# Weight sums of a fast matrix product, formed by adding transfers in device memory instead of on the vector engine, with larger buffer pools and a refitted order of work

## The chip, the cores and the metric

The kernel runs on one core of one Trainium2 chip. The core has five engines with instruction streams of their own: TensorE (PE; its weight loads are listed as PEld), VectorE (DVE), ScalarE (ACT), GpSimd (POOL) and SyncE (SP). SP does nothing here but issue transfers. Transfers issued from SP and ACT go through hardware queues, those from POOL through a software queue; the profile keeps them apart as q1/q10 and q0. The metric is the device time of one execution in microseconds (us). Before the change, three runs gave 1059.16 to 1060.96 us with a median of 1059.97 us.

## The reference

One layer of a bidirectional encoder on 512 tokens of width 1024, all in float32. Two branches read the same normalised input: a gated linear recurrence (RG-LRU, 12 blocks of 128 channels) and a chunked gated delta rule (DeltaNet, 8 heads, with a 64x64 triangular solve in each chunk). Sigmoid gates merge them, and a SwiGLU feed-forward of width 2816 follows.

```python
h = rmsnorm(x, mix_norm)
rx, ry, qkv, z, ba, gates = split(h @ w_in)                 # 1024 x 9248
y_rnn = rglru_branch(rx, ry, ...) @ w_rnn_proj
y_dn  = deltanet_branch(qkv, z, ba, ...) @ w_dn_proj
g_rnn, g_dn = split(sigmoid(gates))
x = x + (g_rnn * y_rnn + g_dn * y_dn) @ w_out
gt, up = split(rmsnorm(x, ffn_norm) @ w_gate_up)             # 1024 x 5632
x = x + (silu(gt) * up) @ w_down                             # 2816 x 1024
return rmsnorm(x, final_norm)
```

The change touches `w_down` above all, and the places where buffers are shared.

## The kernel before, in words

**Precision.** Matrix products run in a one-pass format. Each operand is split into a high part (ACT casts it) and a low part (DVE subtracts it from the original); a product is three matmuls, high by high, high by low and low by high. So every 512 KB block of weights is loaded into a tile `wraw`, cast on ACT into `whi` and subtracted on DVE into `wlo` before PE can use it. Small products of the DeltaNet branch run in plain float32.

**Stages.** In order of time: the norm of the input; the twelve RG blocks (`rg_front`, `rg_mid`, `rg_out`), in which each block also needs four 128x128 gate weights, loaded into a tile `graw` with one buffer; from about 200 to 650 us the DeltaNet pairs g = 0..3 (`dn_front`, `dn_mats`, `dn_inverse`, `dn_state`, `dn_out`), with other projections between them; the output projection; the feed-forward's gate and up products (`gate_up`, about 720 to 950 us); and the down product to the end (`down_first`, `down_second`).

**The fast products.** `gate_up` and the down product use a seven-product scheme on 2x2 blocks (Strassen's, in Winograd's form), which needs sums of weight blocks. For the down product two of them are formed early: for each j of 11, `b11 + b12` and `b12 + b22`. `down_sums(j)` (L1167) loads 512 KB into `bg` and 256 KB into `bgb`, makes two DVE additions of 128x512, and stores the 512 KB result into a DRAM tile `sums[j]`; `down_first(j)` loads it again much later. These calls stand in the loop over `gate_up`.

**The order of work.** Nothing is issued while the functions run. Every operation is recorded (`Rec`, L384, which is why nearly all profile rows carry that line) with its data dependences, a planner's cost and a wished time. `Plan.order` (L145) then walks through a list schedule of the five engines: at each step an engine takes the ready operation of the earliest wished time whose buffers are free. The wished time is the start of the operation's stage, read from the table `TIMES`, plus an offset within the stage. What stands on the chip is the resulting order per engine; there each engine works strictly in that order and waits where it must. Buffers come from shared pools: `two()` of 2 KB per partition (N2 = 14), `four()` of 4 KB (N4 = 22), and NW = 3 `wraw` tiles; `whi` and `wlo` have two each.

**DeltaNet, as far as it is needed.** `dn_mats(g)` reads decays back from DRAM (`t<-gcr`) and masks them on POOL (AFFINE_SELECT); DVE multiplies them into the matrices `na`. `dn_inverse(g)` inverts 32x32 blocks on DVE by a chain of some 60 tiny operations and three transposes; the first 32x32 matmuls (`ax<-t,na`) need its end. `dn_state(g)` runs four chained steps; POOL scales its keys (TENSOR_SCALAR `t<-t,dnse`).

**The tail.** The last matmuls are split into halves of 256 columns, one into an `ax` bank and one into an `st` bank; DVE adds each to the result, squares are summed, the row norm is formed, and the last rows are scaled and written.

Of the kernel before, what the change touches and what calls it, by code (L numbers as in the profile page):

```python
# [8 lines left out]
F32R = mybir.dt.float32r  # L9
AF = mybir.ActivationFunctionType  # L10
ALU = mybir.AluOpType
# [3 lines left out]
P = 128  # L15
D = 1024
# [10 lines left out]
NF = D_FF // P  # L27
# [5 lines left out]
RELEASE = 200  # L33
LOOK = 40
TIMES = [
# [15 lines left out]
]  # L51
ENGINES = ("PE", "DVE", "ACT", "POOL", "SP")
N2, N4, NW = 14, 22, 3
AHEAD = 12.0
LASTK = 3
GATES = (0, 2, 4, 6, 16)
# [333 lines left out]
def trunk(ctx: ExitStack, tc: tile.TileContext, x, mix_norm, w_in, rg_conv_w, rg_conv_b, rg_wa, rg_ba, rg_wx, rg_bx,  # L390
# [3 lines left out]
    plan = Plan(nc)  # L394
    V, A, G, T = Rec(plan, "DVE", nc.vector), Rec(plan, "ACT", nc.scalar), Rec(plan, "POOL", nc.gpsimd), Rec(plan, "PE", nc.tensor)
    Q = Rec(plan, "SP", nc.sync)
# [3 lines left out]
    wp = ctx.enter_context(tc.tile_pool(name="wp", bufs=2))  # L400
# [5 lines left out]
    dr = ctx.enter_context(tc.tile_pool(name="dr", bufs=1, space=DRAM))  # L406
# [4 lines left out]
    def nm(s):  # L411
        uid[0] += 1
        return f"{s}{uid[0]}"

    def new(pool, shape, tag, bufs, dt=F32):
        return plan.tile(pool, shape, dt, tag, bufs, nm(tag))
# [4 lines left out]
    def axb():  # L421
        return new(ps, (P, 512), "ax", 3)
# [4 lines left out]
    def two(dt=F32, shape=(P, 512)):  # L427
        return new(t2, shape, "t2", N2, dt)

    def four(dt=F32, shape=(P, 2, 512)):  # L430
        return new(t4, shape, "t4", N4, dt)
# [7 lines left out]
    def act(out_, in_, func, after=(), **kw):  # L439
        plan.extra = after  # L440
        A.activation(out_, in_, func, **kw)
        plan.extra = ()

    def spend(us=0.0):
        plan.base += us
        plan.t = plan.base
        plan.stage += 1

    def f(ap):
        return ap.bitcast(F32)  # L450
# [112 lines left out]
    def pcol(i, j):  # L563
        return par[:, i, j:j + 1]
# [85 lines left out]
    def split(src, pair):  # L650
        A.copy(pair[:, 0, :], src)
        V.tensor_tensor(pair[:, 1, :], src, f(pair[:, 0, :]), ALU.subtract)
# [83 lines left out]
    wx = rg_wx[0].rearrange("d n k j -> k n d j")  # L736
    yr = [None] * NB

    def rg_front(b):
        u, us, r, i = two(), four(F32R), four(), four()  # L740
        po = in_proj(C_RX + b * P, admit=(u, us, r, i))
        graw, ghi, glo = new(wp, (P, 4, P), "graw", 1), two(F32R, (P, 4, P)), two(F32R, (P, 4, P))
        now = plan.t
        plan.t = now - (40 if b > 2 else 12)
        Q.dma_start(graw[:, 0:2, :], wa[:, b])
        Q.dma_start(graw[:, 2:4, :], wx[:, b])
        plan.t = now - AHEAD
        A.copy(ghi, graw)
        V.tensor_tensor(glo, graw, f(ghi), ALU.subtract)
        plan.t = now  # L750
        conv(po, lambda k: rg_w(k, b), rg_b(b), u)
        split(u, us)
        for q in range(4):
            d = q % 2
            pq = axb()
            T.matmul(pq, ghi[:, q, :], us[:, 0, :], start=True, stop=False)
            T.matmul(pq, ghi[:, q, :], us[:, 1, :], start=False, stop=False)
            T.matmul(pq, glo[:, q, :], us[:, 0, :], start=False, stop=True)
            act((r if q < 2 else i)[:, d, :], pq, AF.Sigmoid, bias=pcol(0, (O_BA if q < 2 else O_BX) + 12 * d + b))
        V.tensor_tensor(i, i, u.unsqueeze(1).to_broadcast([P, 2, S]), ALU.mult)  # L760
        return r, i
# [402 lines left out]
    wdn = w_down[0].rearrange("(j h p) n -> p j h n", p=P, h=2)  # L1164
    sums = {}

    def down_sums(j, after):  # L1167

        now = plan.t
        r, b22 = new(wp, (P, 2, 512), "bg", 2), new(wp, (P, 512), "bgb", 2)  # L1170
        plan.extra = after
        Q.dma_start(r, wdn[:, j, 0, :].rearrange("p (h n) -> p h n", h=2))
        Q.dma_start(b22, wdn[:, j, 1, 512:D])
        plan.extra = ()
        V.tensor_tensor(r[:, 0, :], r[:, 0, :], r[:, 1, :], ALU.add)
        V.tensor_tensor(r[:, 1, :], r[:, 1, :], b22, ALU.add)
        sums[j] = new(dr, (P, 2, 512), "sums", NF // 2)
        Q.dma_start(sums[j], r)
        plan.t = now

    gates = [(rnn_gate, n) for n in range(KD)] + [(dn_gate, n) for n in range(KD)]
    for g in range(4):
        spend()
        dn_mats(g)
        spend()
        dn_inverse(g)
        spend()
        dn_state(g)
        if g < 3:
            dn_z(g)  # L1190
        spend()
        dn_out(g)
        if g < 3:
            dn_front(g + 1)
        if g == 2:
            dn_z(3)
        for fn, n in gates[GATES[g]:GATES[g + 1]]:
            fn(n)
# [9 lines left out]
    for n in range(KD):  # L1208
# [1 line left out]
        y = four(F32R)  # L1210
        split(mixs[n // 2][:, n % 2, :], y)
        mh.append(y)
    last_split = (len(plan.ops) - 1,)
    spend()


# [95 lines left out]
    BRIDGE = 2  # L1312
# [88 lines left out]
        V.tensor_tensor(fa[n // 2][:, n % 2, :], s_, u, ALU.mult)  # L1401

    for n in range(BRIDGE, NF):
        if n - BRIDGE < NF // 2:
            down_sums(n - BRIDGE, last_split)
        gate_up(n)


# [220 lines left out]
```

## Time and profile before

| | before |
|---|---|
| median of three runs | 1059.97 us |
| the profiled execution: its time, from first to last instruction | 1059.7 us |
| mean granted TensorE clock | 0.997 |
| busy PE / DVE / ACT / POOL | 1044.6 / 872.0 / 676.7 / 56.0 us |
| instructions PE / DVE / ACT / POOL | 6731 / 1606 / 1244 / 109 |
| moved by transfers | 122.83 MB |
| transfers of `down_sums` | 11 of 512 KB, 11 of 256 KB, 11 stores of 512 KB |

The program runs on one core, so there is no other core to compare with. A busy PE is not a PE at its peak: the ends of matmuls are modelled and each row includes the pipeline behind it, so a wait shorter than about that pipeline does not show as idle time. The view of waits names, for each engine, the instruction whose end released it.

### The profile page before, as it was taken

How to read it: one execution, taken by the hardware profiler on the slowest of the kernel's cores; microseconds unless marked ns; L12 is line 12 of the kernel's file. 1: busy time of each engine (PE TensorE's matmuls, PEld its weight loads, DVE VectorE, ACT ScalarE, POOL GpSimd, SP SyncE). 2: the span in 40 equal slices, each digit the busy share in tenths (PEclk: the TensorE clock that was granted, in tenths of full speed). 3: DMA queues.
4: the chain of work that ended last, by engine and by line, in shares of the span. 5: the costliest groups of instructions: out<-in, count | busy, mean ns of one | idle time of the engine just before them, and what ended most of it. 6: DMA issues, size and time to landing. Idle time of an engine off the chain costs nothing.

```text
span 1059.7 us, 17669 instructions
## 1 busy us (share of the span) xinstructions
PE 1044.6 (99%) x6731; PEld 909.9 (86%) x6731; DVE 872.0 (82%) x1606; ACT 676.7 (64%) x1244; POOL 56.0 (5%) x109
## 2 busy tenths in 40 slices
PE   8999999999999999999999999999999999999997
PEld 7888887888879887988888798889999999998786
DVE  7679899769876796599489657679999988989998
ACT  7897997887454766874865535447454454545664
POOL 2000000202000230020010000000000000000000
PEclk9999999999999999999999999999999999999999
DMA  8233232233530352224203314566585342435642
GB/s 239 61 109 90 81 104 75 70 110 91 143 94 23 90 148 81 70 60 110 57 20 95 86 33 147 167 211 224 179 249 160 101 119 81 120 100 192 206 139 100
DMA packets 174389, 122.83 MB, mean 116 GB/s; under 512 B 5952, under 2 KB 160720, under 8 KB 174304
## 3 DMA queue, kind: packets, MB, share of 16 engines
q1 hardware_dynamic: 172832, 118.41, 37.4%
q10 hardware_dynamic: 1184, 3.15, 0.8%
q8 instruction: 53, 0.87, 0.4%
q0 software_dynamic: 288, 0.13, 0.1%
q14 instruction: 32, 0.26, 0.1%
HBM read 113.78 MB, written 7.90 MB: 115 GB/s over the span
## 4 chain that ended last, share of the span: by engine, by line
PE 79%; ACT 8%; DVE 7%; DMA 3%; issue 2%; POOL 0%; SPq 0%; DVEq 0%; ACTq 0%; POOLq 0%
PE mm L384 49%; PE ax L384 20%; PE st L384 11%; ACT t L384 5%; DVE t L384 4%; ACT L384 2%; DVE na L384 1%; ACT whi L384 1%; DVE wlo L384 1%; DMA wraw<-in_w_in_dram 1%; DMA wraw<-in_w_gate_up_dram 0%; ACT ax L384 0%; DMA t<-in_x_dram 0%; DMA wraw<-in_w_down_dram 0%; DMA graw<-in_rg_wx_dram 0%
## 5 line engine op out<-in xcount | busy, mean ns | idle before, releaser
L384 DVE TENSOR_TENSOR t<-t,t 128x512 fp32r<-128x512 f32 (+19 forms) x466 | 227.7, 500 | 19.1 <-ACT t L384 10.8
L384 PE MATMUL mm<-hh,whi 128*128 128x512 f32 (+2 forms) x648 | 230.0, 364 | 0.4 <-ACT hh L384 0.3
L384 PE MATMUL mm<-hl,whi 128*128 128x512 f32 (+2 forms) x648 | 229.4, 363 | 0.8 <-DVE hl L384 0.8
L384 ACT CAST whi<-wraw 128x1024 fp32r<-128x1024 f32 (+3 forms) x139 | 129.9, 936 | 129.8 <-PE mm L384 79.1
L384 DVE TENSOR_TENSOR wlo<-wraw,whi 128x1024 fp32r<-128x1024 f32 (+3 forms) x138 | 150.1, 1088 | 70.0 <-ACT whi L384 31.7
L384 PE MATMUL mm<-hh,wlo 128*128 128x512 f32 (+1 forms) x632 | 147.0, 363 | 0.0
L384 PE MATMUL ax<-t,t 32*32 32x32 f32 (+3 forms) x1062 | 140.8, 285 | 1.6 <-issue 1.1
L384 PEld LDWEIGHTS mm<-hl,whi 128*128 128x128 f32 (+1 forms) x648 | 122.0, 188 | 17.9 <-DVE hl L384 1.2
L384 PEld LDWEIGHTS mm<-hh,whi 128*128 128x128 f32 (+1 forms) x648 | 122.0, 188 | 17.8 <-ACT hh L384 0.5
L384 PEld LDWEIGHTS ax<-t,t 128*128 128x128 f32 (+1 forms) x1062 | 109.4, 159 | 19.6 <-issue 2.9
L384 PEld LDWEIGHTS mm<-hh,wlo 128*128 128x128 f32 x632 | 109.1, 189 | 17.3
L384 ACT CAST t<-t 128x512 fp32r<-128x512 f32 (+2 forms) x128 | 81.9, 652 | 49.2 <-DVE t L384 47.3
L384 PE MATMUL mm<-t,t 128*128 128x256 f32 (+1 forms) x468 | 91.3, 336 | 0.1
L384 ACT ACT_TABLE_LOAD x69 | 88.5, 1283 | 3.1 <-PEq L1615 1.7
L384 DVE SCALAR_TENSOR_TENSOR t<-mm,par,t 128x511 f32<-128x511 f32 (+1 forms) x108 | 79.3, 743 | 10.3 <-ACT t L384 9.1
L384 PE MATMUL mm<-t,whi 128*128 128x512 f32 x320 | 83.4, 396 | 0.5 <-ACT whi L384 0.5
L384 PEld LDWEIGHTS mm<-t,t 128*128 128x128 f32 x468 | 72.7, 190 | 9.3 <-DVE t L384 0.5
L384 PEld LDWEIGHTS mm<-t,whi 128*128 128x128 f32 x320 | 59.2, 188 | 13.5 <-ACT whi L384 1.1
L384 ACT ACTIVATE t<-t 128x128 f32<-128x128 f32 (+4 forms) x86 | 47.1, 558 | 27.7 <-DVE t L384 26.2
L384 ACT CAST t<-wraw 128x1024 fp32r<-128x1024 f32 (+1 forms) x51 | 44.9, 881 | 20.8 <-DMA wraw<-in_w_gate_up_dram 11.3
L384 DVE TENSOR_TENSOR t<-wraw,t 128x1024 fp32r<-128x1024 f32 (+1 forms) x51 | 51.3, 1007 | 4.3 <-ACT t L384 4.2
L384 PE MATMUL mm<-t,wlo 128*128 128x512 f32 x160 | 42.7, 393 | 0.0
(210 smaller groups left out, 1704.1 us busy)
## 6 DMA issues: line engine op xcount, KB each, us to landing
wraw<-in_w_in_dram SPq DMA_DIRECT2D x72, 512.0 KB, 3.7
wraw<-in_w_gate_up_dram SPq DMA_DIRECT2D x44, 512.0 KB, 3.8
wraw<-in_w_rnn_proj_dram SPq DMA_DIRECT2D x16, 384.0 KB, 3.5
bg<-in_w_down_dram SPq DMA_DIRECT2D x11, 512.0 KB, 4.5
sums<-bg SPq DMA_DIRECT2D x11, 512.0 KB, 4.2
wraw<-sums SPq DMA_DIRECT2D x11, 512.0 KB, 4.1
wraw<-in_w_down_dram SPq DMA_DIRECT2D x22, 256.0 KB, 2.7
wraw<-in_w_down_dram SPq DMA_DIRECT2D x11, 512.0 KB, 3.6
```

The source lines that it names most:

```text
L384: self.plan.add(e, lambda: real(*a, **kw), outs, ins, cost, tail, table)
```

## The change

Four edits, and a new table of wished times.

1. **Sums by transfers.** `down_sums(j)` no longer uses SBUF or DVE. SP copies the 512 KB of `[b11 | b12]` from the weights in DRAM straight into `sums[j]`, also in DRAM. Then POOL issues two transfers of 256 KB that add (`accum_op=add`): `b12` onto the first half of `sums[j]` and `b22` onto the second, both read from the weights. The two sums are the same as before.
2. **Place.** The calls move from the `gate_up` loop (with a dependence on the last split of the merge) into the DeltaNet loop, three for each pair g, just ahead of `dn_state(g)`.
3. **`graw`.** The gate weights of the RG blocks take a buffer of the 2 KB pool instead of a single tile of their own; their load is planned behind the split of the block before the last one.
4. **Pools.** NW 3 to 4, N4 22 to 24, N2 14 to 16. The tiles `bg` (two of 4 KB), `bgb` (two of 2 KB) and `graw` (one of 2 KB) are gone.

```diff
-N2, N4, NW = 14, 22, 3
+N2, N4, NW = 16, 24, 4
...
+    fronts = []
     def rg_front(b):
         u, us, r, i = two(), four(F32R), four(), four()
         po = in_proj(C_RX + b * P, admit=(u, us, r, i))
-        graw, ghi, glo = new(wp, (P, 4, P), "graw", 1), two(F32R, (P, 4, P)), two(F32R, (P, 4, P))
+        graw, ghi, glo = two(shape=(P, 4, P)), two(F32R, (P, 4, P)), two(F32R, (P, 4, P))
         now = plan.t
         plan.t = now - (40 if b > 2 else 12)
+        plan.extra = fronts[-2:-1]
         Q.dma_start(graw[:, 0:2, :], wa[:, b])
         Q.dma_start(graw[:, 2:4, :], wx[:, b])
+        plan.extra = ()
...
         split(u, us)
+        fronts.append(len(plan.ops) - 1)
...
-    def down_sums(j, after):
-
-        now = plan.t
-        r, b22 = new(wp, (P, 2, 512), "bg", 2), new(wp, (P, 512), "bgb", 2)
-        plan.extra = after
-        Q.dma_start(r, wdn[:, j, 0, :].rearrange("p (h n) -> p h n", h=2))
-        Q.dma_start(b22, wdn[:, j, 1, 512:D])
-        plan.extra = ()
-        V.tensor_tensor(r[:, 0, :], r[:, 0, :], r[:, 1, :], ALU.add)
-        V.tensor_tensor(r[:, 1, :], r[:, 1, :], b22, ALU.add)
-        sums[j] = new(dr, (P, 2, 512), "sums", NF // 2)
-        Q.dma_start(sums[j], r)
-        plan.t = now
+    def down_sums(j):
+
+        sums[j] = new(dr, (P, 2, 512), "sums", NF // 2)
+        plan.extra = (len(plan.ops) - 1,)
+        Q.dma_start(sums[j], wdn[:, j, 0, :].rearrange("p (h n) -> p h n", h=2))
+        plan.extra = ()
+        G.dma_start(sums[j][:, 0, :], wdn[:, j, 0, 512:D], accum_op=ALU.add)
+        G.dma_start(sums[j][:, 1, :], wdn[:, j, 1, 512:D], accum_op=ALU.add)
...
         dn_inverse(g)
         spend()
+        for j in range(3 * g, min(3 * g + 3, NF // 2)):
+            down_sums(j)
         dn_state(g)
...
     for n in range(BRIDGE, NF):
-        if n - BRIDGE < NF // 2:
-            down_sums(n - BRIDGE, last_split)
         gate_up(n)
```

The new `TIMES` changes the order on every engine; PE still issues the same 5962 matmuls. ACT loads its function tables 63 times instead of 69. Three places, in rows of the two programs' orders (a number behind a name tells tiles apart):

POOL at the masks of DeltaNet pair 2. Before (`t_828` to `t_845` are the scaled keys of pair 2, `t_802` to `t_807` its decays):

```order
L384 AFFINE_SELECT t_803<-t_803 128x512
L384 AFFINE_SELECT t_806<-t_806 128x512
L384 AFFINE_SELECT t_807<-t_807 128x512 x2
L384 MEMSET t_946 32x8x32 x2
L384 TENSOR_SCALAR t_828<-t_751,dnse_800 128x128 x4
L384 TENSOR_SCALAR t_836<-t_751,dnse_800 128x128 x4
L384 TENSOR_SCALAR t_845<-t_751,dnse_800 128x128 x4
```

Now (`t_837` to `t_854` are the scaled keys of pair 2, `t_808` and later its decays):

```order
L384 DMA sums_707<-in_w_down_dram 128x512 x2
L384 TENSOR_SCALAR t_837<-t_757,dnse_806 128x128 x4
L384 TENSOR_SCALAR t_845<-t_757,dnse_806 128x128 x4
L384 TENSOR_SCALAR t_854<-t_757,dnse_806 128x128 x3
L384 DMA sums_708<-in_w_down_dram 128x512
L384 AFFINE_SELECT t_808<-t_808 128x512
L384 AFFINE_SELECT t_809<-t_809 128x512
L384 TENSOR_SCALAR t_854<-t_757,dnse_806 128x128
L384 DMA sums_708<-in_w_down_dram 128x512
L384 AFFINE_SELECT t_808<-t_808 128x512
```

The masks of pair 2 now stand behind the first adding transfer of `sums_708`, which waits for the copy into that tile; on SP that copy stands right ahead of the load of `t_808`.

DVE at the end of the inverse of pair 1 (the tiny operations end with the two transposes; `t_692`/`t_691` before and `t_695`/`t_694` now are its working tiles). Before:

```order
L384 TENSOR_TENSOR t_691<-t_691,t_692 128x4x14
L384 TENSOR_TENSOR wlo_885<-wraw_883,whi_884 128x1024
L384 TENSOR_TENSOR t_692<-t_690,t_691 128x42
L384 TENSOR_TENSOR t_691<-t_691,t_692 128x3x14
L384 TENSOR_TENSOR t_692<-t_690,t_691 128x30
L384 TENSOR_TENSOR t_691<-t_691,t_692 128x2x15
L384 TENSOR_TENSOR t_692<-t_690,t_691 128x15
L384 TENSOR_TENSOR t_691<-t_691,t_692 128x15
L384 STREAM_TRANSPOSE t_694<-t_691 128x32x16
L384 TENSOR_TENSOR t_694<-id_136,t_694 128x512
L384 STREAM_TRANSPOSE t_693<-t_694 128x512
```

Now:

```order
L384 SCALAR_TENSOR_TENSOR t_759<-mm_763,par_134,t_759 128x510
L384 TENSOR_TENSOR t_695<-t_693,t_694 128x30
L384 SCALAR_TENSOR_TENSOR t_759<-mm_763,par_134,t_759 128x511
L384 TENSOR_TENSOR t_694<-t_694,t_695 128x2x15
L384 SCALAR_TENSOR_TENSOR t_759<-mm_763,par_134,t_759 128x511
L384 TENSOR_TENSOR t_695<-t_693,t_694 128x15
L384 TENSOR_TENSOR t_694<-t_694,t_695 128x15
L384 STREAM_TRANSPOSE t_697<-t_694 128x32x16
L384 TENSOR_TENSOR t_697<-id_136,t_697 128x512
L384 STREAM_TRANSPOSE t_696<-t_697 128x512
```

The low part of a weight block (`wlo_885`) stood within the last steps; now the three shifted additions of a convolution (`t_759`, which read the product in `mm_763`) do. On PE, what follows that product up to the first 32x32 matmul is now:

```order
L384 MATMUL mm_900<-hh_99,wlo_899 128x512 x8
L384 MATMUL mm_537<-t_488,whi_539 128x512 x2
L384 MATMUL mm_537<-t_494,whi_539 128x512 x2
L384 MATMUL ax_699<-t_696,na_683 32x32
L384 MATMUL ax_699<-t_697,na_683 32x32
```

Ahead of these rows stand 16 more matmuls of `mm_900`, so 28 matmuls of 512 columns lie between the last one of `mm_763` and the first 32x32 one.

DVE in the tail. Before (`ax_1716` and `st_1711` are the banks of the two last halves):

```order
L384 TENSOR_TENSOR na_1130<-ax_1716,na_1130 128x512
L384 TENSOR_TENSOR t_1923<-na_1130,t_1908 128x512
L384 TENSOR_TENSOR na_1130<-st_1711,na_1130 128x256
L384 TENSOR_SCALAR rst_1926<-ssf_1706 128x1
L384 SCALAR_TENSOR_TENSOR t_1925,ssf_1706<-na_1130 128x256
```

Now (`ax_1694` and `st_1689`):

```order
L384 TENSOR_TENSOR t_1901<-na_1141,t_1886 128x512
L384 TENSOR_TENSOR na_1141<-ax_1694,na_1141 128x512
L384 TENSOR_SCALAR rst_1904<-ssf_1684 128x1
L384 TENSOR_TENSOR na_1141<-st_1689,na_1141 128x256
L384 SCALAR_TENSOR_TENSOR t_1903,ssf_1684<-na_1141 128x256
```

On PE the nine matmuls into `ax` were followed by the nine into `st`, which ended the stream; now those into `st` stand more than forty matmuls earlier, and the nine into `ax` end it.

More of the change, by code (lines that the diff above doesn't have):

```diff
@@ L1212, in trunk @@
         mh.append(y)
-    last_split = (len(plan.ops) - 1,)
     spend()
```

30 rows, old and new, of the table TIMES are left out of this document.

## The prediction

> **What bounds the kernel now.** I read the page first: its span and the busy time of the engines.
>
> ```profile
> span 1059.7 us, 17669 instructions
> PE 1044.6 (99%) x6731; PEld 909.9 (86%) x6731; DVE 872.0 (82%) x1606; ACT 676.7 (64%) x1244; POOL 56.0 (5%) x109
> ```
>
> PE is busy for 1044.6 of 1059.7 us, and the change leaves its 5962 matmuls as they are, so the most that any new order can give back is PE's idle time, 15.1 us. Second, the view of waits for PE (engine waited for: us in total, times, longest us), since it says how much of that idle time another engine caused.
>
> ```profile
> PE ax L384 <- DVE ident L384: 2.6, 1, 2.6
> PE ax L384 <- DVE t L384: 2.0, 3, 1.2
> PE ax L384 <- issue: 1.1, 1, 1.1
> PE mm L384 <- DVE hl L384: 0.8, 1, 0.8
> PE mm L384 <- ACT whi L384: 0.5, 1, 0.5
> PE mm L384 <- ACT hh L384: 0.3, 1, 0.3
> PE ax L384 <- ACT t L384: 0.2, 1, 0.2
> PE ax L384 <- DVE na L384: 0.2, 1, 0.2
> ```
>
> They add up to 7.7 us. The first, 2.6 us, is the wait for the identity matrix at the very start, which no part of the change touches: 5.1 us are within reach. Third, the windows, to see where they lie (start:end, length, busy us of PE, PEld, DVE, ACT, POOL with instructions, then granted clock, DMA share, GB/s).
>
> ```profile
> 50.00:100.00 50.00, 49.84 (x219) 40.41 (x218) 42.12 (x49) 45.14 (x61) 0.00 (x0) 1.00 0.33 95
> 400.00:500.00 100.00, 98.80 (x727) 83.85 (x726) 77.09 (x199) 64.88 (x144) 8.52 (x20) 1.00 0.28 77
> 500.00:600.00 100.00, 98.70 (x783) 83.23 (x782) 76.02 (x186) 65.69 (x148) 7.31 (x14) 1.00 0.25 69
> 745.00:905.00 160.00, 159.84 (x1331) 159.56 (x1331) 150.03 (x269) 77.47 (x141) 0.00 (x0) 1.00 0.49 149
> 1005.00:1060.00 55.00, 47.87 (x218) 39.14 (x216) 49.89 (x83) 32.22 (x55) 0.00 (x0) 0.96 0.34 118
> ```
>
> Two thirds of the kernel show PE full; what is missing between 50 us and the tail stands in 400 to 600 us (1.2 + 1.3 us), and the last window lacks 7.1 us, which is the tail behind the last matmul. A limit stands here: matmul ends are modelled, so a short wait inside a busy row does not show.
>
> **The change part by part.** *The DVE additions go.* They ran in the `gate_up` stage (operation, count: ns min/median/max, first to last start).
>
> ```profile
> L384 DVE TENSOR_TENSOR bg<-bg x11: 678/681/686, 709.5 to 808.7; 128x512 f32<-128x512 f32 x11
> L384 DVE TENSOR_TENSOR bg<-bg,bgb x11: 677/681/686, 710.3 to 809.6; 128x512 f32<-128x512 f32 x11
> ```
>
> 22 x 0.681 = 15.0 us of DVE time go. But in the window 745 to 905 us PE is busy for 159.84 of 160 us although DVE is busy for 150.03: the additions were hidden behind the matmuls. Bounds: 0 and the missing 0.16 us. I take **-0.1**. Were that cover gone, the same work would be worth up to the 15.0 us.
>
> *Transfers instead.* The issues of the two ways, and of the load that shares SP with the copy (out<-in, count, size, median us from issue to landing):
>
> ```profile
> sums<-bg SPq DMA_DIRECT2D x11, 512.0 KB, 4.2
> wraw<-sums SPq DMA_DIRECT2D x11, 512.0 KB, 4.1
> t<-gcr SPq DMA_DIRECT2D x16, 256.0 KB, 4.2
> 6.05 0.75 DVE L384 TENSOR_SCALAR t<-t,rin 128x1024 f32<-128x1024 f32 x1
> 5.68 0.52 POOL L384 DMA_DIRECT2D t<-in_rg_lambda_dram  x1
> 6.23 0.70 POOL L384 DMA_DIRECT2D dtb<-in_dn_dt_bias_dram  x1
> L384 SPq DMA_DIRECT2D wraw<-sums x11: 327/371/430, 922.2 to 991.5; - x11
> 398.98 0.97 POOL L384 TENSOR_SCALAR_AFFINE_SELECT t<-t 128x512 f32<-128x512 f32 x1 [3.00 <-ACT t L384]
> 508.07 0.90 PE L384 MATMUL ax<-t,t 32*32 32x32 f32 x82
> ```
>
> The trace of before has no transfer from DRAM to DRAM and none that adds. The copy reads and writes 512 KB: at least a load (4.1), at most a store and a load one after the other (4.2 + 4.1 = 8.3 us). On POOL an issue costs 0.52 to 0.70 us (the last two rows of POOL), 22 of them 11 to 15 us against an engine busy for 56 us. What counts is the wait: POOL works in order, and behind an addition stand keys and masks of the DeltaNet pairs. The copy of `sums_708` is issued on SP right ahead of the load of `t_808`, which needs 4.2 us itself. Two issues on POOL come on top, so the masks are late by the copy's time + 2 x 0.70 - 4.2: 1.3 us for a copy of 4.1, 5.5 us for one of 8.3. 512 KB in 2 KB rows over all 16 engines is nearer the single load, so 1.3. PE pays that only if the masks of pair 2 are on its path. Before, the last of them began at 398.98 us and the first 32x32 work of pair 2 at 508.07, 109 us later; so I let a fifth or so count. The sums are first read at 922.2 us, at least 300 us after the DeltaNet stages in which they are now made, so no reader waits. Bounds 0 and +5.5; I take **+0.3**.
>
> The Trainium skill (page "SBUF — State Buffer", section "🔬 SBUF: two separate sides") speaks against this edit: a transfer issued from GpSimd has its descriptors written by that engine's cores, and these are locked out of a shared port while DVE runs an operation that uses two ports, such as an fp32 copy. This trace agrees weakly: 0.70 us for the POOL issue that lies beside a DVE TENSOR_SCALAR, 0.52 us for the one before it that begins ahead of it. At 0.18 us more for each of 22 issues it would be 4.0 us of POOL time; POOL is idle for 95% of the span, so the sum is the same either way, and only the slower rival below gains. No row here shows an issue held for a whole DVE operation.
>
> *`graw` from the pool, and larger pools.* With one `graw` buffer, a load must wait for the block before (start, us, what, idle before it).
>
> ```profile
> 27.91 0.62 ACT L384 CAST t<-graw 128x512 fp32r<-128x512 f32 x1 [2.58 <-DMA graw<-in_rg_wx_dram]
> 29.07 0.46 PE L384 MATMUL ax<-ident,t 64*128 64x64 f32 x4 [0.19 <-ACT t L384]
> ```
>
> ACT waited 2.58 us for it, and PE 0.19 of that. I take that wait as gone, **-0.2**; later blocks hide theirs behind PE (49.84 of 50 us from 50 to 100). More buffers (NW, N2, N4) can only end a wait for a free one. No PE wait above is for a `wraw` transfer, so they count as 0 here; with the planner's new order they are part of the rearranging below, and nothing becomes late through them.
>
> *Six fewer table loads.*
>
> ```profile
> L384 ACT ACT_TABLE_LOAD x69 | 88.5, 1283 | 3.1 <-PEq L1615 1.7 <-DVE so L384 0.2
> ```
>
> 6 x 1.283 = 7.7 us of ACT, on an engine that is 64% busy. PE waits for ACT are 0.5 + 0.3 + 0.2 = 1.0 us in all; the 0.2 is counted above. Bounds 0 and -0.8; I take **-0.3**, since only a load just ahead of such a wait helps.
>
> *The inverse of pair 1.* The largest DVE wait of PE inside the kernel is its end.
>
> ```profile
> 410.22 1.30 DVE L384 TENSOR_TENSOR t<-t,t 128x42 f32<-128x42 f32 x6
> 411.55 1.20 DVE L384 STREAM_TRANSPOSE t<-t 128x512 f32<-128x512 f32 x1
> 412.78 0.69 DVE L384 TENSOR_TENSOR t<-id,t 128x512 f32<-128x512 f32 x1
> 413.51 0.71 DVE L384 STREAM_TRANSPOSE t<-t 128x512 f32<-128x512 f32 x1
> 414.27 0.75 PE L384 MATMUL ax<-t,na 32*32 32x32 f32 x64 [1.20 <-DVE t L384]
> L384 DVE SCALAR_TENSOR_TENSOR t<-mm,par,t 128x511 f32<-128x511 f32 x72 | 53.1, 743 | 1.0
> L384 ACT ACTIVATE t<-mm,zero_t,par 128x512 f32<-128x512 f32 x24 | 18.6, 778 | 16.4 <-PE mm L384 16.2
> 267.81 40.35 PE mm L384 x178
> ```
>
> Now the order puts 28 matmuls of 512 columns between the product that DVE's convolution reads and the first 32x32 one: 28 x 40.35 / 178 = 6.35 us of PE. In that time ACT evacuates the product (0.78), DVE does three additions of the convolution (3 x 0.743), four tiny steps (4 x 1.30 / 6), the transpose, the addition and the transpose (1.20 + 0.69 + 0.71): 6.48 us, and 0.2 us of hand-offs. PE waits 0.3 us instead of 1.20: **-0.9**. Over the whole inverse, from the products that open it to the first 32x32 matmul, counting both orders with the durations of the trace's groups, PE had 15.2, 6.3, 11.5 and 12.6 us more work than DVE for pairs 0 to 3, and has 7.3, 7.5, 7.6 and 8.3 us now. With 6.3 pair 1 waited 1.20, so hand-offs eat 7.5: every pair now stands at the edge, and pair 0 may wait 0.2. This is inside the +0.3 above.
>
> *The "issue" wait* of 1.1 us precedes pair 2's 32x32 work, and its instructions are rearranged. Bounds 0 and -1.1; the middle, **-0.5**.
>
> *The tail.*
>
> ```profile
> 1051.71 1.24 PE L384 MATMUL st<-t,t 128*128 128x256 f32 x9
> 1051.91 0.69 DVE L384 TENSOR_TENSOR na<-ax,na 128x512 f32<-128x512 f32 x1
> 1053.12 0.42 DVE L384 TENSOR_TENSOR na<-st,na 128x256 f32<-128x256 f32 x1
> ```
>
> The 512-column addition (0.69 us) ran while PE did the nine `st` matmuls; only the 0.42 us one stood behind the last matmul. Now the `ax` matmuls end the stream, and the 0.69 us stand behind it, ahead of the 0.42. **+0.7**.
>
> Sum: -0.1 + 0.3 - 0.2 - 0.3 - 0.9 - 0.5 + 0.7 = -1.0, so 1059.7 becomes 1058.7. That execution lies 0.3 us under the median of the runs, 1059.97; on the scale of the runs the forecast is **1059.0 us**.
>
> **The rivals.** What a measurement of this kernel can tell from no change is about 0.2%, 2.1 us.
>
> *Faster: the new order leaves almost no PE wait.* All of the 5.1 us within reach go, and most of what the matmul model hides: 1059.97 - 5.1 + 0.7 = 1055.6, with a remainder of 0.4 **1056.0**. For it: the waits are few and each is named, and DVE, which causes 3.0 of the 5.1, loses work and tables of ACT go. Against it: in the pairs, where they lie, slack shrinks from 11 to 15 us to under 8.3, and the removed additions were elsewhere.
>
> *Slower: POOL is held by the copy.* If the copy takes 8.3 us, the masks of pair 2 come 5.5 us late; DVE multiplies them in late, the inverse ends late, and its slack of 7.6 us is eaten by the 7.5 of hand-offs, so PE pays all but 0.1: 1059.0 - 0.3 + 5.4 = **1064.1**. It decides from a copy of 6.4 us: 6.4 + 1.4 - 4.2 = 3.6 us late, of which 3.5 are paid, and 1058.7 + 3.5 = 1062.2 is more than 2.1 us over the median. For it: DVE and PE at the edge in all four pairs. Against it: the 109 us by which the masks were ahead before; an order that keeps half of that hides any such copy.
>
> *Slower: the sums aren't ready.* If `wraw<-sums` waited for the additions at 922 us, the down product would start late by at least one landing (4.1 us), 1063.1. With POOL's last addition issued in pair 3's stage I give it almost nothing.
>
> **How the numbers follow.** No measurable change 0.44, with its own range of 1057.9 to 1062.1 (0.2% about the median); almost no waits left 0.34; POOL held 0.20; sums late 0.02. Faster 0.34, same 0.44, slower 0.22. The bounds of all costs reach from 1054.9 (all 5.1 gone) to 1065.5 (+5.5 in full). The range for 8 in 10 leaves out the ends of both: **1055.5 to 1063.5**.
>
> **What would show it.** Right: no DVE row `bg`, and 745 to 905 us no shorter by more than 0.2 us; the first 32x32 matmuls of pair 1 wait under 0.5 us; behind the last matmul an `ax` addition of 0.69 us; copies landing in about 4 to 5 us. Wrong on the slow side: POOL rows waiting for a transfer into `sums`, and PE waiting for DVE at the 32x32 matmuls of pair 2 or 3. Wrong on the fast side: a view of waits for PE with little but the identity, and less idle time in the start or the tail, where I expect none to go.

## The result, and the profile after

The changed kernel takes 1067.47 us (median of 4 runs, 1066.92 to 1068.83) against 1060.47 us for the kernel before on the same chip: a ratio of 1.0066, 95% interval 1.0049 to 1.0083. It is slower by 7.0 us, where 1059.0 and no measurable change were forecast, and it lies above the range. A second measurement, later and beside other kernels, gave 1069.26 us and a ratio of 1.0085 (1.0071 to 1.0099).

The page of the profile after, with busy time by engine and the transfers of the sums:

```profile
span 1065.2 us, 17632 instructions
PE 1045.9 (98%) x6731; PEld 909.5 (85%) x6731; DVE 857.9 (81%) x1584; ACT 669.6 (63%) x1238; POOL 77.1 (7%) x131
sums<-in_w_down_dram SPq DMA_DIRECT2D x11, 512.0 KB, 5.1
sums<-in_w_down_dram POOLq DMA_DIRECT2D x22, 256.0 KB, 5.8
t<-gcr SPq DMA_DIRECT2D x16, 256.0 KB, 5.2
```

What the change was to take away is gone: DVE is busy for 857.9 instead of 872.0 us, ACT for 669.6 instead of 676.7. PE does the same work in 1045.9 us, but the span grew by 5.5 us, and PE's idle time from 15.1 to 19.3 us. The waits of PE after (engine waited for: us in total, times, longest):

```profile
PE ax L384 <- DVE t L384: 5.1, 6, 1.3
PE ax L384 <- DMA gain1r<-in_mix_norm_dram: 3.0, 1, 3.0
PE ax L384 <- ACT t L384: 1.5, 1, 1.5
PE mm L384 <- ACT hh L384: 1.1, 1, 1.1
PE mm L384 <- DVE hl L384: 0.7, 2, 0.4
```

Waits for DVE's `t` rose from 2.0 to 5.1 us, those for ACT from 1.0 to 2.6; the one for "issue" is gone. The first wait at the start, 3.0 us here and 2.6 before, changes from one execution to the next and from kernel to kernel. POOL now waits for transfers into `sums`, one of the signs that the prediction named for the slow side:

```profile
POOL sums L384 <- DMA sums<-in_w_down_dram: 190.4, 6, 64.4
```

The windows (start:end, length, busy us of PE, PEld, DVE, ACT, POOL, then granted clock, DMA share, GB/s) show where it happens:

```profile
300.00:400.00 100.00, 97.96 (x713) 82.60 (x712) 80.21 (x200) 57.23 (x135) 14.78 (x24) 1.00 0.43 107
500.00:600.00 100.00, 98.11 (x721) 82.01 (x720) 72.90 (x180) 59.70 (x135) 10.12 (x18) 1.00 0.37 94
600.00:700.00 100.00, 99.03 (x708) 82.42 (x707) 62.41 (x118) 47.36 (x92) 3.28 (x4) 1.00 0.48 136
745.00:905.00 160.00, 159.96 (x1333) 159.76 (x1332) 141.45 (x251) 77.63 (x141) 0.00 (x0) 1.00 0.34 100
```

Two of the same stretches before:

```profile
300.00:400.00 100.00, 100.00 (x723) 84.19 (x723) 74.35 (x159) 64.91 (x150) 15.31 (x26) 1.00 0.32 89
600.00:700.00 100.00, 100.00 (x654) 83.97 (x653) 59.69 (x113) 44.78 (x85) 0.00 (x0) 1.00 0.37 114
```

PE is full in the stage from which the DVE additions went (159.96 of 160 us, before 159.84). It has holes in 300 to 400 and 600 to 700 us, where before it had none, and at 500 to 600 us: in the DeltaNet stages, into which the transfers moved, and right behind them. The granted clock is 1.00 in all of these windows.

### The profile page after: what moved, and what is told of

Read it like the earlier page. It is cut to its first block, busy times and chain, and to the rows that moved or that the text cites. A ratio compares the mean times of both kernels' runs of the same rounds, so it can differ in the third digit from the quotient of the medians.

```text
span 1065.2 us, 17632 instructions
## 1 busy us (share of the span) xinstructions
PE 1045.9 (98%) x6731; PEld 909.5 (85%) x6731; DVE 857.9 (81%) x1584; ACT 669.6 (63%) x1238; POOL 77.1 (7%) x131
## 4 chain that ended last, share of the span: by engine, by line
PE 86%; DVE 9%; ACT 1%; DMA 1%; issue 1%; SPq 0%; POOL 0%; DVEq 0%; ACTq 0%; POOLq 0%
PE mm L384 49%; PE ax L384 23%; PE st L384 14%; DVE t L384 6%; DVE wlo L384 2%; DVE na L384 1%; DMA wraw<-in_w_gate_up_dram 1%; ACT t L384 1%; DMA t<-gcr 0%; ACT ax L384 0%; SPq L384 0%; DMA t<-in_rg_wx_dram 0%; ACT L384 0%; DVE nq L384 0%; ACT hh L384 0%
## 5 line engine op out<-in xcount | busy, mean ns | idle before, releaser
L384 DVE TENSOR_TENSOR t<-t,t 128x512 fp32r<-128x512 f32 (+23 forms) x478 | 235.3, 503 | 34.6 <-ACT t L384 25.8
L384 PE MATMUL ax<-t,t 32*32 32x32 f32 (+3 forms) x1062 | 138.4, 286 | 1.2 <-DVE t L384 1.2
L384 ACT CAST t<-t 128x512 fp32r<-128x512 f32 (+2 forms) x140 | 89.3, 650 | 68.3 <-DVE t L384 61.3
```

What stands on the lines that cost most here:

```text
L384: self.plan.add(e, lambda: real(*a, **kw), outs, ins, cost, tail, table)
```

## The experiments

Two theories stood at first. **Order**: the new table of wished times lays waits on PE's path, and the transfers cost nothing. **Transfers**: the copies and additions delay something, and the order is harmless. All runs are timed in five rounds beside the kernel before on the same chip. The runs of the last four rows were made on another chip than the other experiments; the kernel before has medians of 1060.14 to 1060.23 us in all of these series.

| kernel | median us | ratio to before, 95% interval |
|---|---|---|
| the change, first and second measurement | 1067.47, 1069.26 | 1.0066 (1.0049–1.0083), 1.0085 (1.0071–1.0099) |
| the change without transfers into `sums` | 1064.45 | 1.0041 (1.0027–1.0055) |
| before, sums by transfers | 1060.53 | 1.0006 (0.9997–1.0015) |
| the change with the old table | 1064.05 | 1.0042 (1.0029–1.0054) |
| before with the new table | 1087.09 | 1.0256 (1.0242–1.0270) |
| the change, copies only | 1063.70 | 1.0034 (1.0022–1.0047) |
| the change, additions moved | 1063.87 | 1.0037 (1.0024–1.0051) |
| the change, old tail | 1066.41 | 1.0063 (1.0051–1.0076) |
| additions moved, one cast later | 1062.27 | 1.0023 (1.0014–1.0033) |
| additions moved, three repairs | 1060.93 | 1.0003 (0.9995–1.0012) |
| before, sums by transfers, three additions between keys | 1063.99 | 1.0042 (1.0029–1.0054) |
| before, sums by transfers, low part later | 1059.93 | 0.9998 (0.9989–1.0007) |

**The change without its transfers.**

```diff
         for i in todo:
-            plan.ops[i][1]()
+            fn = swap.get(i, plan.ops[i][1])    # None for copies and additions
+            if fn is not None:
+                fn()
```

> The change with its order kept on PE, DVE and ACT instruction for instruction, but without the 11 copies and 22 adding transfers; the down product loads the plain weights in place of the sums, so two of the seven products get unsummed weights. Order theory (the new table of wished times lays waits on PE's path; the transfers cost nothing): about 1067, within 1.5 us of the change's 1067.5, with the same PE waits at 321, 354, 503, 642 and 702 us. Transfer theory (copies and additions delay loads, or hold POOL or SP): 1060 to 1062, and the waits at 503 and 702 us gone.

1064.45 us: neither theory alone. Without the transfers, 3.0 to 4.8 us of the change's loss go (against its two measurements), and about 4 us stay. So both hold in part. The two kernels run the same instructions on DVE, PE and ACT in the same order, so rows can be laid side by side. In the change, at 350 us (start, us, engine, what, and idle time before it):

```profile
349.76 3.12 POOL L384 TENSOR_SCALAR t<-t,dnse 128x128 f32<-128x128 f32 x6 [11.74 <-DVE dnse L384]
352.83 0.74 POOL L384 DMA_DIRECT2D sums<-in_w_down_dram  x1
353.41 2.25 POOL L384 TENSOR_SCALAR t<-t,dnse 128x128 f32<-128x128 f32 x6
353.40 1.79 DVE L384 TENSOR_SCALAR nq<-nq 128x8 f32<-128x8 f32 x1
355.93 1.13 PE L384 MATMUL ax<-t,t 128*128 128x128 f32 x8 [1.20 <-DVE t L384]
```

and the same DVE and PE instructions without the transfers:

```profile
353.23 0.21 DVE L384 TENSOR_SCALAR nq<-nq 128x8 f32<-128x8 f32 x1
354.39 1.06 PE L384 MATMUL ax<-t,t 128*128 128x128 f32 x8
```

An operation of 128x8 elements takes 1.79 us where it takes 0.21 without the addition that POOL issued just ahead of it. PE then waits 1.20 us. POOL itself did not wait there. The waits of PE at 323, 502, 568 and 641 us (0.8, 0.5, 0.5 and 1.0 us) stand without the transfers too, so they belong to the order; those at 354 and 703 us are gone. This made a third theory, **port**: while POOL prepares an adding transfer, DVE is held.

**Before, with the sums by transfers.** The order of before on all engines; copies at the start of each `dn_state` on SP, additions on POOL one pair later.

```diff
+            for j in group(g) if g >= 0 else ():
+                nc.sync.dma_start(sums[j], wdn[:, j, 0, :].rearrange("p (h n) -> p h n", h=2))
+            for j in [*group(g - 1), *(group(3) if g == 3 else ())] if g > 0 else ():
+                nc.gpsimd.dma_start(sums[j][:, 0, :], wdn[:, j, 0, 512:D], accum_op=ALU.add)
+                nc.gpsimd.dma_start(sums[j][:, 1, :], wdn[:, j, 1, 512:D], accum_op=ALU.add)
+            if i not in swap:     # loads, DVE additions and stores of down_sums left out
+                plan.ops[i][1]()
```

> The kernel before with its order and buffers kept, but the sums by transfers: no loads, additions and stores of down_sums, the copies of three j at the start of each dn_state on SP, the additions on POOL one pair later. Order theory: 1060, within 1 us of before (the 15 us of DVE additions were hidden). Transfer theory: 1064 to 1067.

1060.53 us: no measurable difference from before. Forming the sums by transfers is free and worth nothing, as the additions stand here: in groups behind POOL's masks or keys, with nothing behind them on POOL for at least 13 us.

**The two tables.** Each structure with the other's table of wished times (only `TIMES` replaced).

> The change with the wished times of before (both tables have 229 entries). Order theory: another order, so another time; a table fitted to other pools and another place of the sums need not fit, 1062 to 1075, with the waits at other places than in the change. Transfer theory: it stays 6 us or more above before whatever the table.

> The kernel before with the change's table of wished times: its own pools, place and DVE additions. Order theory: clearly slower than before, 1065 or more, since the table alone lays the waits. Transfer theory: within 2 us of before.

1064.05 us: with the table of before the change is faster than with the one made for it. 1087.09 us: the new table on the old structure costs 27 us; PE's products wait 10.4 us for DVE's `t` there, and not at all for it before.

```profile
PE mm L384 <- DVE t L384: 10.4, 4, 8.4
PE mm L384 <- ACT whi L384: 5.5, 3, 2.7
```

The order alone is worth more here than anything that the change adds or removes. The transfer theory's numbers for these two (6 us or more whatever the table; within 2 us) are both out.

**Copies only, and additions moved.** First, the 22 additions left out:

```diff
+        skip = {i for a in adds.values() for i in a}
         for i in todo:
-            plan.ops[i][1]()
+            if i not in skip:
+                plan.ops[i][1]()
```

> The change without the 22 additions but with the 11 copies, so the two weight sums lack their second terms. Port theory: as without any transfer, 1064.5 within 1. Traffic theory: halfway, about 1066, since the copies move 11.5 MB (read and write) and the additions 17.3 MB (two reads and a write).

Then all transfers kept, but the first nine pairs of additions put behind the last masks and the last keys in POOL's order:

```diff
+        late = {pool[-13]: moved[:12], pool[-1]: moved[12:]}   # pool: POOL's order without the additions
         for i in todo:
-            plan.ops[i][1]()
+            if i not in moved:
+                plan.ops[i][1]()
+            for k in late.get(i, ()):
+                plan.ops[k][1]()
```

> The change with the adding transfers moved on POOL alone: those of the first six sums behind the last mask of pair 3, those of the next three behind the last keys, where no DVE TENSOR_SCALAR and no POOL work waits. Copies, PE, DVE, ACT and SP orders as in the change. Port theory (POOL's writing of an addition's descriptors holds DVE): DVE's TENSOR_SCALAR at 353 us back to 0.2 us, the PE wait at 354 gone, 1.2 to 3 us faster than the change: 1064.5 to 1066.3. Traffic theory (the bytes of the transfers slow other loads): no change, 1067.5 within 1.

And the change itself again, for a second profile and on the same chip:

> The change itself once more, with a second profile. If the PE wait at 354 us (1.2) comes from the addition issued on POOL between the keys, it is there again, with the DVE TENSOR_SCALAR beside it again over 1.5 us. If the wait at 702 us (1.5, a load that landed after 6.2 us) is the chance of one execution, it is gone or elsewhere; if it belongs to the order, it is there again. Time 1067.5 within 1.

The copies cost nothing measurable (1063.70 against 1064.45 without any transfer), and neither do the additions when moved (1063.87): 3.6 us less than the change's first measurement, 5.4 less than the one beside it. The traffic theory expected no gain from moving them. (Against the first measurement alone the intervals still touch, against the one beside it they are apart.) The view of the tile `nq` (ns min/median/max) in the change's second profile, with the additions moved, and, from a later run, with three additions put between keys in the order of before:

```profile
L384 DVE TENSOR_SCALAR nq<-nq x4: 160/162/1798, 191.8 to 548.8; 128x8 f32<-128x8 f32 x4
```

```profile
L384 DVE TENSOR_SCALAR nq<-nq x4: 160/160/197, 191.7 to 546.3; 128x8 f32<-128x8 f32 x4
```

```profile
L384 DVE TENSOR_SCALAR nq<-nq x4: 161/288/2803, 215.6 to 539.7; 128x8 f32<-128x8 f32 x4
```

The 1.8 us are there in both profiles of the change (1.79, 1.80) and gone when the additions move. A second loss goes with them. In the change, the masks of pair 2 wait for their loads between the additions, and the first 32x32 matmul of pair 2 is late:

```profile
454.65 0.82 POOL L384 DMA_DIRECT2D sums<-in_w_down_dram  x1
458.29 2.74 POOL L384 TENSOR_SCALAR_AFFINE_SELECT t<-t 128x512 f32<-128x512 f32 x4 [0.59 <-DMA t<-gcr]
461.35 1.22 POOL L384 TENSOR_SCALAR_AFFINE_SELECT t<-t 128x512 f32<-128x512 f32 x2 [0.32 <-DMA t<-gcr]
504.62 0.57 PE L384 MATMUL ax<-t,na 32*32 32x32 f32 x44 [1.31 <-DVE t L384]
DMA to landing us min/median/max: 1.5/5.1/7.6
```

and with the additions moved (the last line of either fence is the landing time of the loads `t<-gcr`; its minimum is the one store into `gcr`):

```profile
455.65 6.90 POOL L384 TENSOR_SCALAR_AFFINE_SELECT t<-t 128x512 f32<-128x512 f32 x10 [2.31 <-ACT t L384]
502.41 0.75 PE L384 MATMUL ax<-t,na 32*32 32x32 f32 x64 [0.54 <-DVE t L384]
DMA to landing us min/median/max: 1.5/4.5/5.8
```

The loads land after up to 7.6 us instead of 5.8, the masks come 0.8 us later, and some 40 us on, at the end of the inverse, PE waits 1.31 instead of 0.54 (2.12 in the change's second profile). DVE carries the 0.8 us there: it waits for POOL's masks at 462 and 464 us (0.28 and 0.33), not so with the additions moved, and from then on its rows lie 2.2 us behind those of the kernel with the additions moved, where they lay 1.4 behind. The difference in landing is not wide: the longest of these loads takes 8.2 us in the second profile, and 6.2 with copies only and 6.5 without any transfer.

**The old tail.** The change, with the last 118 operations in the order of before.

```diff
+        n = len(plan.ops)
+        todo = [i for i in todo if i < n - len(TAIL)] + [n + k for k in TAIL]
```

> The change with the last 118 operations in the order that they have in the kernel before, so that the nine matmuls into st end PE's stream again and the 512-column addition runs beside them. By the tail's term of the prediction 0.7 us faster than the change, 1066.8; by the profiles (7.8 us from the last matmul to the end against 7.0) the same. If other work at the end was placed to use the gap, no gain or a loss of up to 1.

1066.41 us, 2.8 less than the change on the same chip and 1.1 less than its first measurement; the intervals of the ratios overlap, so the time alone does not settle 0.7 us. In the profiles it is plain: from the start of the last matmul to the end of the span there are 6.9 us with the old tail, 7.8 in the change and 7.1 before.

**One cast later.** With the additions moved, ACT's cast of the first gate weights goes behind the six casts of `hh`.

```diff
+        acts = [k for k in todo[todo.index(casts[0]) + 1:] if plan.ops[k][0] == "ACT"]
+        todo = shift(todo, casts[0], acts[5])     # directly behind acts[5]
```

> The kernel with the additions moved, and one instruction more moved: ACT's cast of the first RG block's gate weights stands behind the six casts of hh instead of ahead of them. Order theory: ACT no longer waits for that load ahead of hh (0.5 to 1.1 us in the profiles) nor does the 0.6 us cast in front of it; PE's wait for hh at 11 us falls from 1.3 to about 0.2, and the time by 1.1: about 1062.8. Rival: another start condition (the load of the next weights, DVE's hl) takes its place, no gain: 1063.9.

1062.27 us, 1.6 less than without this move (the intervals of the ratios overlap a little, and the chip is another). The start of ACT and PE without it:

```profile
10.26 0.62 ACT L384 CAST t<-t 128x512 fp32r<-128x512 f32 x1 [0.50 <-DMA t<-in_rg_wx_dram]
10.79 2.29 ACT L384 ACTIVATE hh<-ax,gain 128x256 fp32r<-128x256 f32 x6
11.31 0.33 PE L384 MATMUL mm<-hh,whi 128*64 128x256 f32 x1 [1.34 <-ACT hh L384]
```

and with it:

```profile
9.91 2.30 ACT L384 ACTIVATE hh<-ax,gain 128x256 fp32r<-128x256 f32 x6
12.05 0.66 ACT L384 CAST t<-t 128x512 fp32r<-128x512 f32 x1
10.44 0.33 PE L384 MATMUL mm<-hh,whi 128*64 128x256 f32 x1 [0.30 <-ACT hh L384]
```

At 28 us the same matmul of PE starts 1.5 us earlier with the move. Waits explain 0.65 of it: the one for `hh` is 1.04 us shorter, the one for DVE's `hl` behind it 0.39 longer (0.83 instead of 0.44). The rest is the granted clock of TensorE, 0.57 without the move and 1.00 with it from 13 to 17 us:

```profile
13.00:17.00 4.00, 4.00 (x24) 4.00 (x23) 4.00 (x12) 3.88 (x10) 0.00 (x0) 0.57 1.15 304
13.00:17.00 4.00, 4.00 (x34) 3.77 (x32) 3.48 (x10) 3.39 (x9) 0.00 (x0) 1.00 1.13 296
```

Whether the longer wait brings the lower clock is not shown: the profile of the kernel before has 0.74 in this window with a wait of only 0.31 us for `hh`, and the same start in the kernel before with the sums by transfers has 1.00.

**Three repairs.** That move, the old tail, and the low part `wlo` that stands in the inverse of pair 0 put behind its last transpose.

```diff
+        end = turns[0]            # last transpose of the inverse of pair 0
+        low = [k for k in todo[:todo.index(end)] if plan.ops[k][0] == "DVE" and not heads[0] <= k <= end][-1]
+        todo = shift(todo, low, end)
```

> The kernel with the additions moved, with three repairs of the order: the cast behind hh, the low part of a weight block behind the last transpose of the inverse of pair 0 instead of ahead of it, and the tail in the order of before. Order theory: 1063.9 less 1.1, less 0.97 (the wait at 322 us), less 0.7 to 1: about 1061.0, within 1 of before; what is left are the waits at 503, 568 and 640 us. Rival (the waits pass on to the next chain): 1062.5 to 1064.

1060.93 us, as forecast by the order theory (the two rearrangements added here are worth 1.3), and no longer different from before by this measurement. In the change these rows stood at pair 0; with the repair the 32x32 matmul waits for nothing, though 0.34 us come back at the next step of the same chain:

```profile
321.05 1.22 DVE L384 TENSOR_TENSOR wlo<-wraw,whi 128x1024 fp32r<-128x1024 f32 x1
322.18 0.70 DVE L384 STREAM_TRANSPOSE t<-t 128x512 f32<-128x512 f32 x1
322.94 0.75 PE L384 MATMUL ax<-t,na 32*32 32x32 f32 x64 [0.85 <-DVE t L384]
```

```profile
319.99 0.75 PE L384 MATMUL ax<-t,na 32*32 32x32 f32 x64
322.45 1.02 PE L384 MATMUL ax<-t,t 32*32 32x32 f32 x96 [0.34 <-ACT t L384]
```

**Additions between keys, in the order of before.** The counter-test of the port theory: the harmless kernel with three of its 22 additions moved between POOL's keys.

```diff
+        early = {keys[12 + 7]: 0, keys[24 + 7]: 1, keys[36 + 2]: 3}    # behind the 8th key of pairs 1 and 2, the 3rd of pair 3
...
+            if i in early:
+                j = early[i]
+                nc.gpsimd.dma_start(sums[j][:, 0, :], wdn[:, j, 0, 512:D], accum_op=ALU.add)
```

> The kernel before with the sums by transfers, with three of the 22 additions put between POOL's keys of pairs 1, 2 and 3, shortly ahead of DVE's TENSOR_SCALAR on nq. Port theory: that TENSOR_SCALAR, 0.16 to 0.38 us there, takes over 1 us at two or three of the places, and keys behind the addition 0.5 instead of 0.37; PE pays 0 to 1.4 for each, 0.5 to 3 us in sum: 1061 to 1063.5. Rival (the 1.8 us were particular to the change's order): DVE rows unchanged, 1060.5.

1063.99 us, 3.5 more than with these three additions elsewhere. That is a little more than the port theory forecast (1061 to 1063.5), and far from its rival's 1060.5; its rows came only in part. At pair 2 it shows fully:

```profile
451.25 0.72 POOL L1620 DMA_DIRECT2D sums<-in_w_down_dram  x1
452.36 2.80 DVE L384 TENSOR_SCALAR nq<-nq 128x8 f32<-128x8 f32 x1
455.81 1.13 PE L384 MATMUL ax<-t 128*128 128x256 f32 x4 [1.76 <-DVE t L384]
374.73 1.81 POOL L384 TENSOR_SCALAR_AFFINE_SELECT t<-t 128x512 f32<-128x512 f32 x3 [4.55 <-DMA t<-gcr]
386.90 1.39 PE L384 MATMUL mm<-t,whi 128*128 128x512 f32 x5 [0.97 <-DVE t L384]
```

At pair 1 (the last two rows) the TENSOR_SCALAR took only 0.34 us, but the load for the masks came late: POOL waited 4.55 us for it, 2.75 without the addition, and PE paid 0.97 us twelve us later. At pair 3 the TENSOR_SCALAR took only 0.23, but the low part that comes 1.5 us later on DVE took 2.20 us, where the kernel without the move has 1.21:

```profile
538.93 0.79 POOL L1620 DMA_DIRECT2D sums<-in_w_down_dram  x1
541.19 2.20 DVE L384 TENSOR_TENSOR wlo<-wraw,whi 128x1024 fp32r<-128x1024 f32 x1
```

So an addition hurts in two ways: a DVE operation is held beside it, and a load beside it is late. Which operation is held depends on a us or two.

What holds DVE is narrower than the port theory says. In every one of these rows POOL went straight on from the addition to keys, and the rows of these keys grew from 0.37 to between 0.51 and 0.62 us (1.6 for the last two of pair 3), one overlapping the next. At pair 1 keys followed too and nothing was held, so it also takes the right operation beside them. Keys without an addition ahead of them leave the TENSOR_SCALAR at 0.20 to 0.39 us. And additions without keys behind them hold nothing: where the additions are moved, nine stand in a row, and the same kind of low part beside them takes its usual time.

```profile
481.21 7.64 POOL L384 DMA_DIRECT2D sums<-in_w_down_dram  x9
486.28 1.22 DVE L384 TENSOR_TENSOR wlo<-wraw,whi 128x1024 fp32r<-128x1024 f32 x1
```

So the runs show that an addition with keys right behind it holds DVE. Whether the preparing of the transfer does it, or the keys that it slows, is not settled.

**The low part later, in the order of before.** The counterpart of the pair-0 repair, at pair 1.

```diff
+        end = turns[1]
+        low = [k for k in todo[:todo.index(end)] if plan.ops[k][0] == "DVE" and not heads[1] <= k <= end][-1]
+        todo = shift(todo, low, end)
```

> The kernel before with the sums by transfers, and the low part of a weight block (1.22 us on DVE) that stood in the inverse of pair 1 moved behind its last transpose. By the prediction's term for that inverse the wait of 1.20 us at 414 goes: 1.0 less than with it, about 1059.5, and under before by 0.6 to 1. Rival: the block's product waits for its low part instead, 1060.5.

1059.93 us. Waits for DVE `t` fall to 1.0 us, and the one at 412 us is gone:

```profile
PE ax L384 <- DVE t L384: 1.0, 2, 0.6
```

But against before (0.9989 to 1.0007) or the kernel without the move (1060.53) the time is not resolved. No version here is measurably faster than the kernel before.

## Why the prediction was wrong, point by point

**The bound held.** PE was full, and no edit could give more than its idle time. The forecast went wrong on what the new work and the new order would take, not on what the removed work was worth.

- *The DVE additions, -0.1.* Right. The stage shows 159.96 of 160 us, and the kernel before without them is unchanged (1060.53).
- *The transfers, +0.3 of a possible +5.5.* **This is the step that failed most.** The price of the copy was right in kind: it lands after 5.1 us, near the single load (4.1) and far from 8.3, and copies alone cost nothing. The step asked only how long POOL would wait for the copy, and let a fifth of that count because the masks of before were 109 us early. Moving the additions showed 3.6 to 5.4 us. The cost was not POOL's waiting. It was a DVE operation held for 1.6 us beside an addition (PE paid 1.20), and loads of the decays that landed late beside others (PE paid 0.8 in the first profile, 1.6 in the second). The 109 us were read in the order of before; in the new one the inverse of pair 2 used its masks as soon as they came. These two rows give 2.0 and 2.8 us; most of what else lies between the profiles is the wait at 703 us, which is left open below.
- *The rival of the held POOL.* It named the engine, pair 2's masks, and 1064.1 us. By its own terms it did not decide: it needed a copy of 6.4 us, and the copy ahead of pair 2's masks took 5.2. Both signs that the prediction named for the slow side came, PE's wait at the 32x32 matmuls of pair 2 (1.31) and POOL's waits for transfers into `sums` (190.4 us). But these waits cost nothing: behind each of them POOL's next keys wait another 8 to 12 us for DVE, or there are none left, and at pair 2's masks POOL did not wait for the copy. Its place was right, its mechanism was another. The rule on the shared port that the prediction cites was set aside because POOL is idle for 95% of the span, so that a longer issue could not matter. It looked at what DVE does to POOL; the loss came from what POOL does to DVE.
- *`graw`, -0.2.* Right: the wait at 29 us is gone, though one of 0.3 us for DVE's `hl` stands at 28 us. But the new table also moved a cast of these weights ahead of `hh` on ACT, so ACT waited for its load where PE waits for ACT. The sum has no term for that; moving the cast back gave 1.6 us. It is the table's doing and not that of the buffer: the change with the old table has the cast behind `hh` and no wait for `hh`, and the kernel before with the new table, with its single `graw`, has the cast ahead and waits 1.20 us.
- *Six fewer table loads, -0.3.* They are gone (63 instead of 69), but PE's waits for ACT did not fall in sum: 1.0 us before, 2.6 after. The 0.5 for `whi` and the 0.2 for `t` went; 1.1 for the `hh` above and 1.5 at 703 us came. The gain of the table loads alone was not measured.
- *The inverse, -0.9.* Right for pair 1: its first 32x32 matmuls, at 409.65 us in the change, show no idle time ahead of them, where 1.20 us were and 0.3 was predicted. The count that put every pair at the edge allowed 0.2 us more; with the additions moved, pair 0 waits 0.81 and pair 2 0.54. Two waits of PE at transposes (`ax<-ident,t`) at 569 and 642 us, 0.5 and 1.0, are new with this order too, and the sum has no term for them. The count of whole work between two points does not see a low part between the last two transposes.
- *The "issue" wait, -0.5.* Gone in full (1.1) in the change; 0.2 to 0.5 us of such a wait come back with the additions moved.
- *The tail, +0.7.* Right: 7.8 instead of 7.1 us behind the start of the last matmul.
- *A reading.* What is missing between 50 us and the tail does not all stand in 400 to 600 us: from 100 to 200 us PE lacks 0.6 us (99.44 of 100), most of it the wait for `whi`. The sum does not change by it.

By runs, the loss of 7.0 us (9.1 in the second measurement) is made up so: 3.6 to 5.4 for where the additions stand, 1.6 for the cast, 1.3 for the tail and pair 0 together, and 0.8 that can't be told from nothing. These add up to 7.3 and 9.1; the 0.3 is the difference between two medians of the kernel before. Each is a difference of medians, good to a us or so, since executions of one kernel here lie up to 3.6 us apart.

**Left open.** A wait of PE at 700 us, behind a weight load that landed after 6.2 us, is 1.5 us in the change and 1.7 in its second profile, 0.6 with the additions moved, 0.2 with the old tail (and the additions in place), 0.2 with the cast later, and none with the three repairs, without transfers or with copies only. It is not tied to the additions by these runs.

## What to carry to other kernels

Where the bounding engine is full, removing hidden work gives nothing, and the risk of a change is in where its new instructions stand; so look at each engine's neighbours of a new instruction, not at its idle share. A transfer issued from GpSimd is work on that engine: put it where neither more work of its own queue nor a short VectorE operation on a tight chain is due. A table that sets the order should be judged by time on the chip: here the old table served the changed kernel better than the one made for it.

## What the runs showed of the hardware

- With an adding transfer of 256 KB issued on POOL and POOL's keys right behind it, a DVE TENSOR_SCALAR of 128x8 took 1.79, 1.80 and 2.80 us, where it takes 0.16 to 0.57 elsewhere, and in one place a TENSOR_TENSOR of 128x1024 took 2.20 instead of 1.21. Other additions, beside other DVE operations, held none, so the length of the hold is not given by these runs. The Trainium skill ("SBUF — State Buffer", section "🔬 SBUF: two separate sides") calls the port pair that DVE and GpSimd share an exclusive lock: a GpSimd operation, or a DVE operation in a two-port mode or (against a GpSimd operation that reads SBUF) with two SBUF inputs, whichever starts first, holds it for its whole instruction. These rows agree with that in the direction that the section's warning does not name, POOL holding DVE.
- POOL's masks hold DVE as well, by less: without any transfer, a low part of 128x1024 (TENSOR_TENSOR) that began 0.1 us behind an AFFINE_SELECT took 1.66 us; the same instruction took 1.22 in the change, where no mask stood beside it.
- In the change, copying 512 KB from DRAM to DRAM landed after 5.1 us (median of 11), adding 256 KB onto DRAM after 5.8 us (median of 22); one issue of an addition took 0.69 to 1.22 us on POOL. Where nine additions stand in a row, their rows overlap and reach 3.0 us, and they land after 4.5 to 13.8 us.
